# Compressed-cache page loads of a decoder step: eight page numbers per register load, whole pages, pages queued ahead of weight slabs

## The chip, the cores and the metric

One Trainium2 chip, and one of its cores. The metric is device microseconds of the whole program, from launch to the last output, as the median of several runs. A profiled execution of the same program gives the trace from which all rows below are read.

## What is computed

The program is one inference step of a small decoder layer for a prompt of 512 tokens and for 8 sample sequences of 4 tokens, all in float32. The change touches only one part of it: the compressed branch of the sample group's attention, which reads 8 pages of a paged cache per sequence and compresses them with a small network.

```python
def compress(rows, pe, w1, w2):
    halves = pad(rows).reshape(b, nc + 1, CMP_STRIDE, g, d)
    blocks = concatenate([halves[:, :-1], halves[:, 1:]], axis=2) + pe[:, None, :]
    flat = blocks.transpose(0, 1, 3, 2, 4).reshape(b, nc, g, CMP_BLOCK * d)
    return gelu(flat @ w1) @ w2

def full_rows(cache, new):                     # page_table: 8 sequences x 8 pages
    rows = cache[page_table].reshape(b, past, 2, N_KV, HEAD_DIM)
    ...
kc, vc = compress_kv(full_rows(cache_cmp, kv_cmp), pe, w1, w2)
```

A second job of the same stretch is the modulation of the layer's norms, `silu(c) @ w_ada + b_ada`, whose weight comes in 24 slabs of 1 MB. After it come the input projection, the attention, and the feed-forward network, which make up nine tenths of the time.

## The kernel before

Every float32 product is made of three passes on TensorE: a value is split into a high part (ScalarE, `ACTIVATE`) and the remainder (VectorE, `TENSOR_TENSOR`), and high by high, high by low and low by high are added up.

**The sixteen stages.** The loop over `n` (line 553) has 16 stages. Stage `n` works on sequence ("batch") `b = n // 2`, with its keys for even `n` and its values for odd `n`. A batch is 8 pages of 256 KB, one `gt` tile of 2 MB. For a stage, `cmp_split` makes two `xh` tiles on ScalarE and two `xl` tiles on VectorE out of `gt`; `cmp_M` then runs 48 matmuls (`phi`, lines 507 to 509); `cmp_finish` adds the bias on ScalarE (`t`, line 515) and applies gelu (`h`, line 519), and `cmp_out2` makes a small product `ph`. Between stages stand the modulation products `modp` (line 285), each of one slab `ada`, and their transposes `modq`. Ahead of stage 0 stand dummy matmuls (`wake`, line 539) and a bias product `pb` (line 434).

**Tiles.** `gt` tiles have few places: batches 0 and 3 share one, 1 and 4 another, 2, 5 and 7 a third, and batch 6 takes two of the three places for slabs (`raw`). A tile's load can start only when the batch before it in the same place has been split. Weight slabs `phi` and `ada` go through the three `raw` places in turn.

**The SP queue.** All these loads are DMAs issued by SyncE (SP), in one order that is written out by hand: `queue()` (line 208) ties every DMA behind the one before it (`tc.issue_after`), until `ordered` is cleared at stage 11. A page number must be in a register of SP before its page can be issued. `page()` (line 462) loads one number at a time from the SBUF tile `pti`, which has the page table in all 128 partitions, asserts its range, works out the address, and issues the DMA. The DMAs use eight semaphores in turn, so each DMA waits for the landing of the eighth before it. The order is: page table, slab `phi 0`, `hp` (biases, small weights), the first halves (keys) of batch 0's pages, slab `phi 1`, the second halves, `hd`, batch 1, slab `ada 0`, batch 2, slabs `ada 1` and `ada 2`, `xT` (2.2 MB), slab `ada 3`, batch 3, and so on.

**The order on the other engines** is made by a scheduler from the dependences and from its own estimate of times; it isn't written in the code. Each engine then runs its instructions strictly in that order.

Of the kernel before, what the change touches and what calls it, by code (L numbers as in the profile page):

```python
# [142 lines left out]
def build(tc, a, o):  # L143
# [64 lines left out]
    def queue(f):  # L208

        if not ordered[0]:  # L210
            return f()
        if last_q[0] is None:
            last_q[0] = f()
        else:
            with tc.issue_after(last_q[0].ins):
                last_q[0] = f()
        return last_q[0]
# [189 lines left out]
    ptf = mp.tile([128, 64], F32, name="ptf")  # L407
    pm_ = mp.tile([128, 64], F32, name="pm_")
    fidx = mp.tile([128, 8], F32, name="fidx")
    queue(lambda: sync.dma_start(pti, a["page_table"].rearrange("(x b) g -> x (b g)", x=1).broadcast_to([128, 64])))  # L410

    p0 = ExitStack()
    wphip = mkpool(p0, "wphi", side="right")
# [33 lines left out]
    ccv = a["cache_cmp"].rearrange("(n p) w -> n p w", p=128)  # L447
    gb_ = {}

    def cmp_gather(b, vs=(0, 1)):  # L450


        if b not in gb_:
            if b == 6:
                gb_[b] = [raw_tile("gt6").rearrange("p (j w) -> p j w", j=4) for _ in range(2)]
            elif b in (2, 5, 7):
                gb_[b] = [gat.tile([128, 8, 512], F32, tag="gt", bufs=1, name=nm("gt"))]
            else:
                gb_[b] = [hpool.tile([128, KC * NT], F32, tag="h" + "hl"[b in (1, 4)], bufs=1, name=nm("gt"))[:, 0:4096].rearrange("p (j w) -> p j w", j=8)]
        cs = slice(256 * vs[0], 256 * vs[-1] + 256)  # L460

        def page(pg):
            t = gb_[b][pg // 4][:, pg % 4, cs] if b == 6 else gb_[b][0][:, pg, cs]
            r = sync.value_load(pti[0:1, b * 8 + pg:b * 8 + pg + 1], min_val=0, max_val=N_PHYS - 1)
            return sync.dma_start(t, ccv[bass.ds(r, 1)].rearrange("n p w -> (n p) w")[:, cs])

        for pg in range(8):
            queue(lambda: page(pg))

    xst = ExitStack()  # L470
    xp = mkpool(xst, "xp", side="right")
    xT = xbig("xT")
    phi_load(0)
    queue(lambda: sync.dma_start(hp, a["hp"]))
    cmp_gather(0, (0,))
    phi_load(1)
    cmp_gather(0, (1,))
    queue(lambda: sync.dma_start(hd, a["hd"]))
    cmp_gather(1)
    adas = [slab("ada", 0)]  # L480
    cmp_gather(2)
    act.activation(cT[:, :, 0:9], c_in.rearrange("p (k n) -> p k n", k=8), AF.Silu)

    last_hi, last_lo = [None], [None]
# [61 lines left out]
    accs1 = [xp.tile([128, HW[hf]], F32, name=f"xacc{hf}") for hf in range(2)]  # L546
    fin_, mods = None, []
    xs_ = [cmp_split(0, 0, hc) for hc in range(2)]
    wake(2)
    pool.memset(vext[32:64], 0.0)  # L550
    units = []
    AHEAD = {0: (1,), 1: (2,), 2: (3,), 3: (4,), 4: (5,), 5: (6,), 9: (7,)}
    for n in range(16):
        b, v = n // 2, n % 2
        if n == 0:
            with tc.issue_after(last_hi[0].ins):
                for qt in range(4):
# [12 lines left out]
        if n in MODS:  # L570
            mod_slab(MODS.index(n), adas[MODS.index(n)])
        for s_ in AHEAD.get(n, ()):
            adas.append(slab("ada", s_))
        if n == 1:
            queue(lambda: sync.dma_start(xT.rearrange("p k n -> p (k n)"), a["xT"]))
        if n in (2, 4, 6, 8, 11):
            cmp_gather({2: 3, 4: 4, 6: 5, 8: 6, 11: 7}[n])
        if n == 11:
            ordered[0] = False
        if 5 <= n < 9:  # L580
            with tc.issue_after(last_hi[0].ins):
                for k in (2 * n - 10, 2 * n - 9):
                    for hf in range(2):
                        square_acc(xT, k, hf, accs1[hf], xp, k == 0)
        if n == 9:
            invs = [inv_bcast(inv_from_sums(tok_sums(accs1[hf], hf, xp), xp), hf, xp) for hf in range(2)]
        if n == 11:
            modp.pop()()
            make_A(n1T, sc1, A1)
            h = hh_, hl_ = tuple(hpool.tile([128, KC, NT], F32R, tag="h" + n_, bufs=1, name="h_" + n_) for n_ in "hl")  # L590
            units = [u for hf in range(2) for u in [modulate(xT, invs[hf], A1, sh1, hh_, hl_, hf, xp)] * KC]
        for _ in range(3 if n < 15 else 4):
            if units:
# [887 lines left out]
```

## Time and profile before

| | us |
|---|---|
| median of 3 runs (lowest, highest) | 1327.63 (1326.82, 1328.21) |
| the profiled execution, its own time | 1327.7 |
| span from its first to its last instruction | 1325.9 |
| TensorE busy in the span | 1293.4 |
| VectorE busy | 641.5 |
| ScalarE busy | 542.8 |

TensorE is busy for 98% of the span, so a gain must come from where it isn't, or from where it works at its lower clock. The granted clock is given as a share of full speed: 1.00 is 2.4 GHz and 0.50 is 1.2 GHz. Both kinds of loss lie almost wholly in the first 90 us, in the stages above. Outputs of other views name an engine's sequencer with a q (SPq), "PEld" is the loading of weights into TensorE, and "idle before" is the time for which an engine stood still ahead of an instruction, with what ended it.

### The profile page before, as it was taken

What the parts mean: (1) busy time and instruction counts of PE and PEld (TensorE: products, weight loads), DVE (VectorE), ACT (ScalarE), POOL (GpSimd) and SP (SyncE); (2) the same over time, 40 slices, a digit from 0 to 9 for tenths busy, and PEclk for the clock granted to TensorE, in tenths of its full rate; (3) what the DMA queues carried; (4) which work ended last, traced back from release to release, by engine and by line L of the source; (5) the groups of instructions that cost most, each with busy time, mean ns of one, the idle gap of its engine ahead of it and who ended that gap; (6) DMA issues with size and microseconds to landing.
All of it is one profiled execution on the core that took longest, in us unless ns stands there. A gap on an engine that the chain in (4) does not pass through costs nothing.

```text
span 1325.9 us, 26272 instructions
## 1 busy us (share of the span) xinstructions
PE 1293.4 (98%) x10950; PEld 1208.0 (91%) x10950; DVE 641.5 (48%) x1553; ACT 542.8 (41%) x1070; POOL 54.8 (4%) x105
## 2 busy tenths in 40 slices
PE   6999999999999999999999999999999999999997
PEld 4889999998898998998778778999999999999996
DVE  3347632344355454336668576667333333333335
ACT  4346543333232335126677676445323222222223
POOL 1000120001111010001000000000000000000000
PEclk8899999999999999999999999999999999999998
DMA  5975146663755543834536334331123122122211
GB/s 179 360 251 172 68 145 228 223 210 108 278 210 211 223 159 129 210 120 136 150 128 200 108 103 179 127 128 65 64 70 122 64 96 96 56 88 88 88 65 68
DMA packets 43398, 191.39 MB, mean 144 GB/s; under 512 B 4980, under 2 KB 12532, under 8 KB 26904
## 3 DMA queue, kind: packets, MB, share of 16 engines
q1 hardware_dynamic: 40832, 163.52, 36.6%
q0 software_dynamic: 2448, 26.19, 5.1%
q8 instruction: 86, 1.41, 0.4%
q14 instruction: 32, 0.26, 0.1%
HBM read 174.49 MB, written 23.54 MB: 149 GB/s over the span
## 4 chain that ended last, share of the span: by engine, by line
PE 91%; DMA 3%; SPq 2%; DVE 1%; issue 1%; ACT 1%; POOL 0%; POOLq 0%; DVEq 0%; ACTq 0%
PE lin L236 19%; PE lin L237 19%; PE lin L238 19%; PE dn L238 3%; PE dn L236 3%; PE dn L237 3%; PE acc L1164 3%; PE ptp L1170 3%; PE phi L507 2%; PE modp L285 2%; PE phi L508 2%; PE phi L509 2%; DMA wraw<-in_cache_win 2%; PE kt L881 2%; PE sp L1139 1%
## 5 line engine op out<-in xcount | busy, mean ns | idle before, releaser
L232 DVE TENSOR_TENSOR wl<-raw,wh 128x1024 fp32r<-128x1024 f32 (+1 forms) x148 | 178.7, 1207 | 261.4 <-ACT wh L231 260.9
L231 ACT ACTIVATE wh<-raw 128x1024 fp32r<-128x1024 f32 (+1 forms) x148 | 154.9, 1047 | 332.6 <-PE lin L237 238.7
L236 PE MATMUL lin<-h_h,wh 128*128 128x288 f32 x976 | 286.8, 294 | 0.0
L238 PE MATMUL lin<-h_h,wl 128*128 128x288 f32 x976 | 281.4, 288 | 0.0
L237 PE MATMUL lin<-h_l,wh 128*128 128x288 f32 x976 | 280.9, 288 | 0.0
L237 PE MATMUL lin<-h_lo,wh 128*128 128x288 f32 (+1 forms) x672 | 193.9, 289 | 0.0
L238 PE MATMUL lin<-h_hi,wl 128*128 128x288 f32 (+1 forms) x672 | 193.4, 289 | 0.0
L236 PE MATMUL lin<-h_hi,wh 128*128 128x288 f32 (+1 forms) x672 | 192.7, 287 | 0.0
L236 PEld LDWEIGHTS lin<-h_h,wh 128*128 128x128 f32 x976 | 183.8, 188 | 9.5 <-issue 8.3
L237 PEld LDWEIGHTS lin<-h_l,wh 128*128 128x128 f32 x976 | 183.9, 188 | 0.4
L238 PEld LDWEIGHTS lin<-h_h,wl 128*128 128x128 f32 x976 | 183.7, 188 | 0.3
L236 PEld LDWEIGHTS lin<-h_hi,wh 128*128 128x128 f32 x672 | 126.8, 189 | 0.0
L237 PEld LDWEIGHTS lin<-h_lo,wh 128*128 128x128 f32 x672 | 126.5, 189 | 0.2 <-DVE h_lo L361 0.2
L238 PEld LDWEIGHTS lin<-h_hi,wl 128*128 128x128 f32 x672 | 126.1, 188 | 0.0
L236 PE MATMUL dn<-f_hi,wh 128*128 128x256 f32 (+1 forms) x352 | 101.7, 289 | 0.0
L238 PE MATMUL dn<-f_hi,wl 128*128 128x256 f32 (+1 forms) x352 | 101.5, 288 | 0.0
L237 PE MATMUL dn<-f_lo,wh 128*128 128x256 f32 (+1 forms) x352 | 101.1, 287 | 0.0
L507 PE MATMUL phi<-xh,wph 128*128 128x256 f32 x256 | 77.4, 302 | 9.8 <-ACT xh L494 9.8
L508 PE MATMUL phi<-xl,wph 128*128 128x256 f32 x256 | 75.9, 296 | 3.1 <-DVE xl L495 3.1
L1146 ACT ACTIVATE P<-P,nms 128x512 f32<-128x512 f32 (+3 forms) x128 | 70.7, 555 | 19.6 <-DVE nms L1145 18.7
L509 PE MATMUL phi<-xh,wpl 128*128 128x256 f32 x256 | 75.1, 294 | 0.0
L1145 DVE CUSTOM_DVE_ANT_0 P<-sp,ta 128x512 f32<-128x512 f32 (+3 forms) x128 | 57.6, 482 | 30.1 <-PE sp L1133 22.4
(349 smaller groups left out, 2381.6 us busy)
## 6 DMA issues: line engine op xcount, KB each, us to landing
raw<-in_wt SPq DMA_DIRECT2D x98, 1024.0 KB, 4.9
gt<-in_cache_cmp SPq DMA_DIRECT2D x56, 256.0 KB, 3.2
wraw<-in_cache_win POOLq DMA_DIRECT2D x8, 1024.0 KB, 8.7
out_new_win_sample<-in_cache_win SPq DMA_DIRECT2D x8, 512.0 KB, 5.8
out_new_win_sample<-in_cache_win SPq DMA_DIRECT2D x8, 504.0 KB
raw<-in_wt SPq DMA_DIRECT2D x4, 768.0 KB, 4.2
xT<-in_xT SPq DMA_DIRECT2D x1, 2176.0 KB
x<-in_xT SPq DMA_DIRECT2D x1, 2176.0 KB
```

Source lines behind the costliest of these rows:

```text
L231: act.activation(oh, view, AF.Copy)
L232: dve.tensor_sub(ol, view, oh.bitcast(F32))
L236: pe.matmul(p, lhsT=wh[:, k, :], rhs=xh, start=start, stop=False)
L237: pe.matmul(p, lhsT=wh[:, k, :], rhs=xl, start=False, stop=False)
L238: pe.matmul(p, lhsT=wl[:, k, :], rhs=xh, start=False, stop=stop)
L507: pe.matmul(ps_, lhsT=w_h, rhs=mh, start=(ch == 0 and s == 0), stop=False)
L508: pe.matmul(ps_, lhsT=w_h, rhs=ml, start=False, stop=False)
L509: pe.matmul(ps_, lhsT=w_l, rhs=mh, start=False, stop=(ch == 7 and s == 1))
L1145: dve.tensor_tensor_reduce(out=t[:, 0:n], in0=sps[br], in1=t_dist[:, 512 - n:512], scale=-hs, scalar=3e38, op0=ALU.add, op1=ALU.min, accum ...
L1146: act.activation(t[:, 0:n], t[:, 0:n], AF.Exp, scale=-1.0, bias=nms[:, c:c + 1], accum_out=sums[:, c:c + 1])
L1164: pe.matmul(acc[br * 64:br * 64 + 64, :], lhsT=vtok[br][:, j, g * 64:(g + 1) * 64], rhs=pts_[br], start=(j == 0), stop=False)
L1170: pe.transpose(tp[:, r * 128:(r + 1) * 128], P[br, r][:, 128 * j:128 * j + 128], ident)
```

## The change

- `page()` is gone. `cmp_gather` loads the eight page numbers of a batch with one instruction into eight registers, without range assertions.
- The page numbers for this come from a new tile `ptr`, one partition of 64 numbers, loaded first. The broadcast of the table into all 128 partitions (`pti`), which stage 15 still needs, is queued later, behind batch 2.
- Batch 0 is loaded as 8 whole pages, ahead of slab `phi 1`, no longer as 16 half pages around it.
- Batches 3, 4 and 5 are issued at stages 1, 3 and 5 (before: 2, 4 and 6), and ahead of the `ada` slab of the same stage. `xT` is queued at stage 2 (before: 1).
- There is one more dummy matmul (`wake(3)` for `wake(2)`).

```diff
+    ptr = mp.tile([1, 64], I32, name="ptr")
+    ptv = a["page_table"].rearrange("(x b) g -> x (b g)", x=1)
+    queue(lambda: sync.dma_start(ptr, ptv))
...
-        def page(pg):
-            t = gb_[b][pg // 4][:, pg % 4, cs] if b == 6 else gb_[b][0][:, pg, cs]
-            r = sync.value_load(pti[0:1, b * 8 + pg:b * 8 + pg + 1], min_val=0, max_val=N_PHYS - 1)
-            return sync.dma_start(t, ccv[bass.ds(r, 1)].rearrange("n p w -> (n p) w")[:, cs])
-
+        with tc.issue_after(last_q[0].ins):
+            ld, regs = nc.values_load_multi_w_load_instructions(ptr[:, b * 8:b * 8 + 8], [mybir.EngineType.SP], min_val=0, max_val=N_PHYS - 1, skip_runtime_bounds_check_because="a page table names pages of the cache")
+        last_q[0] = ld[-1]
         for pg in range(8):
-            queue(lambda: page(pg))
+            t = ts[pg // 4][:, pg % 4] if b == 6 else ts[0][:, pg]
+            queue(lambda: sync.dma_start(t, ccv[bass.ds(regs[pg], 1)].rearrange("n p w -> (n p) w")))
...
-    cmp_gather(0, (0,))
+    cmp_gather(0)
     phi_load(1)
-    cmp_gather(0, (1,))
     queue(lambda: sync.dma_start(hd, a["hd"]))
     cmp_gather(1)
     adas = [slab("ada", 0)]
     cmp_gather(2)
+    queue(lambda: sync.dma_start(pti, ptv.broadcast_to([128, 64])))
...
-    wake(2)
+    wake(3)
...
-        for s_ in AHEAD.get(n, ()):
-            adas.append(slab("ada", s_))
-        if n == 1:
+        if n in (1, 3, 5, 8, 11):
+            cmp_gather({1: 3, 3: 4, 5: 5, 8: 6, 11: 7}[n])
+        if n in AHEAD:
+            adas.append(slab("ada", AHEAD[n]))
+        if n == 2:
             queue(lambda: sync.dma_start(xT.rearrange("p k n -> p (k n)"), a["xT"]))
-        if n in (2, 4, 6, 8, 11):
-            cmp_gather({2: 3, 4: 4, 6: 5, 8: 6, 11: 7}[n])
```

What this does to the order on the engines is shown at three places. First SP at the start of the program, from the first slab to the first page; `gt_147` and `gt_148` are batch 0's tile. Before:

```order
L222 DMA raw_144<-in_wt 128x2048
L474 DMA hp<-in_hp 128x264
L464 TENSOR_LOAD pti
L464 ISA x2
L465 ISA
L465 DMA gt_147<-in_cache_cmp 128x256
```

With the change:

```order
L222 DMA raw_145<-in_wt 128x2048
L473 DMA hp<-in_hp 128x264
L463 TENSOR_LOAD ptr
L467 ISA
L467 DMA gt_148<-in_cache_cmp 128x512
```

Before, the four rows from the load to the DMA stand for each of the 72 pages and half pages; now the load stands once per batch, and a page has one `ISA` row (the address) and its DMA, which moves 512 columns and not 256.

Second, SP from the last page of batch 2 to the first of batch 3 (`gt_805` and `gt_466`). Before:

```order
L465 DMA gt_394<-in_cache_cmp 128x512
L222 DMA raw_617<-in_wt 128x2048
L222 DMA raw_708<-in_wt 128x2048
L575 DMA xT<-in_xT 128x4352
L222 DMA raw_803<-in_wt 128x2048
L464 TENSOR_LOAD pti
L464 ISA x2
L465 ISA
L465 DMA gt_805<-in_cache_cmp 128x512
```

With the change:

```order
L467 DMA gt_205<-in_cache_cmp 128x512
L480 DMA pti<-in_page_table 128x64
L222 DMA raw_375<-in_wt 128x2048
L463 TENSOR_LOAD ptr
L467 ISA
L467 DMA gt_466<-in_cache_cmp 128x512
```

Between the two batches there were three slabs and `xT`, and there are now the small broadcast and one slab; the other two slabs and `xT` follow behind batch 3.

Third, ScalarE where it passes from the bias and gelu of one stage to the split of a later one. Before, around the split of stage 6 (`xh_1212`, `xh_1216`); `t_78` is the bias of stage 5, which reads the end of that stage's matmuls:

```order
L287 ACTIVATE m_72_1064<-modp_1047 128x128
L515 ACTIVATE t_78_1206<-phi_1153,pbias 128x256
L183 ACTIVATE kcs_91<-ph_77_1202 128x2x63
L519 ACTIVATE h_79_1210<-t_78_1206 128x252
L494 ACTIVATE xh_1212<-gt_805 128x1024
L494 ACTIVATE xh_1216<-gt_805 128x1024
```

With the change, around the split of stage 8 (`xh_1067`, `xh_1071`); `t_105` is the bias of stage 7:

```order
L514 ACTIVATE t_93_982<-phi_927,pbias 128x256
L327 ACTIVATE sq_1002<-xT 128x288
L327 ACTIVATE sq_1005<-xT 128x256
L518 ACTIVATE h_94_986<-t_93_982 128x252
L514 ACTIVATE t_105_1061<-phi_1008,pbias 128x256
L493 ACTIVATE xh_1067<-gt_679 128x1024
L493 ACTIVATE xh_1071<-gt_679 128x1024
```

Before, a stage's split stood behind the end of the stage just ahead of it at stage 6; stage 6 is now split earlier (its `xh` stands ahead of the bias of stage 4), and the place where a split stands behind the end of the stage just ahead of it is stage 8. From stage 13 on, the order on TensorE is the same in both kernels.

## Rows read from the trace of the kernel before

**Rows 1.** The page: busy time of each engine, share of the span, instructions.

```profile
PE 1293.4 (98%) x10950; PEld 1208.0 (91%) x10950; DVE 641.5 (48%) x1553; ACT 542.8 (41%) x1070; POOL 54.8 (4%) x105
```

**Rows 2.** Stages: stretch, length, busy (count) per engine, granted clock, DMA share, GB/s.

```profile
17.30:24.30 7.00, 6.26 (x27) 5.97 (x28) 5.06 (x7) 3.15 (x6) 0.00 (x0) 0.50 0.59 200
...
31.10:38.00 6.90, 6.15 (x27) 5.86 (x28) 2.36 (x2) 1.13 (x3) 0.00 (x0) 0.51 0.83 287
...
44.70:48.30 3.60, 3.60 (x41) 3.22 (x41) 2.30 (x3) 0.94 (x2) 0.00 (x0) 0.53 0.81 303
48.30:75.40 27.10, 27.10 (x298) 25.25 (x296) 7.76 (x18) 7.54 (x14) 0.00 (x0) 1.00 1.01 391
...
79.20:82.40 3.20, 3.12 (x38) 2.42 (x38) 3.09 (x5) 2.89 (x6) 0.00 (x0) 0.51 0.98 341
```

**Rows 3.** TensorE's waits from 0 to 110 us: total, times, longest.

```profile
PE phi L507 <- ACT xh L494: 9.8, 4, 5.5
PE phi L508 <- DVE xl L495: 3.1, 4, 0.9
...
PE ph L527 <- ACT h L519: 1.2, 1, 1.2
PE pbt L441 <- DVE pbs L436: 0.5, 1, 0.5
```

**Rows 4.** TensorE in order of time: start, length, what, idle before and its releaser.

```profile
9.84 1.98 PE L539 MATMUL wake<-ident 128*128 128x512 f32 x4
17.36 0.58 PE L507 MATMUL phi<-xh,wph 128*128 128x256 f32 x1 [5.54 <-ACT xh L494]
...
23.48 0.41 PE L509 MATMUL phi<-xh,wpl 128*128 128x256 f32 x1
23.69 0.41 PE L507 MATMUL phi<-xh,wph 128*128 128x256 f32 x1
...
24.70 0.29 PE L507 MATMUL phi<-xh,wph 128*128 128x256 f32 x1
24.82 0.28 PE L508 MATMUL phi<-xl,wph 128*128 128x256 f32 x1
...
78.02 0.39 PE L507 MATMUL phi<-xh,wph 128*128 128x256 f32 x1 [2.20 <-ACT xh L494]
79.28 0.58 PE L508 MATMUL phi<-xl,wph 128*128 128x256 f32 x1 [0.87 <-DVE xl L495]
...
95.73 0.37 PE L507 MATMUL phi<-xh,wph 128*128 128x256 f32 x1
```

**Rows 5.** SP in order of time: the issues of eight pages (the first two: half pages).

```profile
6.01 8.26 SPq L465 DMA_DIRECT2D gt<-in_cache_cmp  x8
...
15.53 8.70 SPq L465 DMA_DIRECT2D gt<-in_cache_cmp  x8
...
25.48 8.40 SPq L465 DMA_DIRECT2D gt<-in_cache_cmp  x8
```

**Rows 6.** Lines 464 and 465: duration in ns (lowest/median/highest); DMA to landing.

```profile
L464 SPq TENSOR_LOAD <-pti x72: 263/268/476, 5.0 to 120.5; - x72
...
L465 SPq DMA_DIRECT2D gt<-in_cache_cmp x72: 332/333/1219, 6.0 to 121.3; - x72
...
DMA to landing us min/median/max: 2.0/3.2/13.7
```

**Rows 7.** ScalarE and VectorE in order of time, as in rows 4.

```profile
7.84 1.15 ACT L427 ACTIVATE wph<-raw 128x512 fp32r<-128x512 f32 x2 [5.82 <-DMA raw<-in_wt]
...
16.25 2.00 ACT L494 ACTIVATE xh<-gt 128x1024 fp32r<-128x1024 f32 x2 [4.64 <-DMA gt<-in_cache_cmp]
...
17.34 1.23 DVE L495 TENSOR_TENSOR xl<-gt,xh 128x1024 fp32r<-128x1024 f32 x1 [4.93 <-ACT xh L494]
```

**Rows 8.** The DMA view from 48 to 75 us: what was moved.

```profile
DMA packets 2867, 10.56 MB, mean 391 GB/s; under 512 B 319, under 2 KB 319, under 8 KB 2193
```

**Rows 9.** The chain that ended last, its first piece.

```profile
0.75 4.24 DMA pti<-in_page_table
```

More of the change, by code (lines that the diff above doesn't have):

```diff
@@ L409, in build @@
     fidx = mp.tile([128, 8], F32, name="fidx")
-    queue(lambda: sync.dma_start(pti, a["page_table"].rearrange("(x b) g -> x (b g)", x=1).broadcast_to([128, 64])))
+    ptr = mp.tile([1, 64], I32, name="ptr")
+    ptv = a["page_table"].rearrange("(x b) g -> x (b g)", x=1)
+    queue(lambda: sync.dma_start(ptr, ptv))
     p0 = ExitStack()
@@ L448, in build, with cmp_gather @@
     gb_ = {}
[L450 to L460, printed above, removed]
-        def page(pg):
-            t = gb_[b][pg // 4][:, pg % 4, cs] if b == 6 else gb_[b][0][:, pg, cs]
-            r = sync.value_load(pti[0:1, b * 8 + pg:b * 8 + pg + 1], min_val=0, max_val=N_PHYS - 1)
-            return sync.dma_start(t, ccv[bass.ds(r, 1)].rearrange("n p w -> (n p) w")[:, cs])
+    def cmp_gather(b):
+        if b == 6:
+            ts = [raw_tile("gt6").rearrange("p (j w) -> p j w", j=4) for _ in range(2)]
+        elif b in (2, 5, 7):
+            ts = [gat.tile([128, 8, 512], F32, tag="gt", bufs=1, name=nm("gt"))]
+        else:
+            ts = [hpool.tile([128, KC * NT], F32, tag="h" + "hl"[b in (1, 4)], bufs=1, name=nm("gt"))[:, 0:4096].rearrange("p (j w) -> p j w", j=8)]
+        gb_[b] = ts
+        with tc.issue_after(last_q[0].ins):
+            ld, regs = nc.values_load_multi_w_load_instructions(ptr[:, b * 8:b * 8 + 8], [mybir.EngineType.SP], min_val=0, max_val=N_PHYS - 1, skip_runtime_bounds_check_because="a page table names pages of the cache")
+        last_q[0] = ld[-1]
         for pg in range(8):
-            queue(lambda: page(pg))
+            t = ts[pg // 4][:, pg % 4] if b == 6 else ts[0][:, pg]
+            queue(lambda: sync.dma_start(t, ccv[bass.ds(regs[pg], 1)].rearrange("n p w -> (n p) w")))
     xst = ExitStack()
@@ L548, in build @@
     xs_ = [cmp_split(0, 0, hc) for hc in range(2)]
-    wake(2)
+    wake(3)
     pool.memset(vext[32:64], 0.0)
     units = []
-    AHEAD = {0: (1,), 1: (2,), 2: (3,), 3: (4,), 4: (5,), 5: (6,), 9: (7,)}
+    AHEAD = {0: 1, 1: 2, 2: 3, 3: 4, 4: 5, 5: 6, 9: 7}
     for n in range(16):
```

## The prediction

> **What bounds the kernel now.** I read the page first: TensorE is busy for 1293.4 of 1325.9 us [rows 1], so the end moves only by what TensorE is idle or slow. The stage table and TensorE's waits then show where that is. In the first 110 us it waits 9.8 us for `xh`, 3.1 us for `xl`, 1.2 and 0.5 us for small products [rows 3]: 14.6 us. The gaps are 5.54 us ahead of stage 0 and 2.20 + 0.87 us at stage 6 [rows 4]; the rest lies ahead of stages 1 and 2.
>
> The second loss is the clock. In four stretches, 17.3 to 24.3, 31.1 to 38.0, 44.7 to 48.3 and 79.2 to 82.4 us, the granted clock is 0.50 to 0.53, that is the 1.2 GHz level, and each follows one of those gaps [rows 2, 4]. At that level two matmuls of a stage start 0.21 us apart, at 2.4 GHz 0.12 us [rows 4], so 0.43 of the busy time there is lost. Busy are 6.26 + 6.15 + 3.60 + 3.12 = 19.1 us [rows 2]; 0.43 of that is 8.2, and I take 8.0, since the first matmul after a gap is long for another reason. Idle and slow together are 22.6 us. That is all this change can reach.
>
> Why it waits: SP. It issues eight half pages in 8.3 us, eight more in 8.7, then batch 1 in 8.4, one after the other until 33.9 us [rows 5]: 1.1 us a page, of which the DMA itself is 0.33 and the load of its number 0.27 [rows 6]. Batch 1 is the data of stage 2. When SP has slots and the queue is full, the engines move 391 GB/s [rows 8], and 200 to 303 GB/s in the first three slow stretches [rows 2]. So up to stage 5 issue is the limit, not the memory.
>
> **Page numbers.** A page now costs an address and a DMA. Its spacing lies between 0.33 us (the DMA alone) and 1.1 us (as now) [rows 5, 6]; without load (0.27) and assertion, with one address row for three, I take 0.5, nearest to the DMA. One load per batch brings eight numbers. Its price is between 0.27 us, one load, and 8 x 0.268 = 2.14 us [rows 6]; I take the nearer row, one instruction out of SBUF, 0.27. The Trainium skill (Runtime: NRT & Kernel Launch, "Instruction fetch mechanics") speaks against this half of the change: a load costs about 200 ns for each register, in bulk too. By it the load would take an estimated 1.6 us, stage 0 would run some 0.8 us later and the sum would be 1311.8; no run here shows a load of eight.
>
> The saving, about 8 x 0.6 = 5 us of SP per batch, is on the path only until the DMA engines are full. A batch of 2.10 MB takes 5.4 us at 391 GB/s [rows 8], longer than its issue (0.3 + 8 x 0.5 = 4.3). From then on memory sets the pace, and what lies ahead of a page in the queue counts in bytes.
>
> **The table as one row.** The broadcast of 128 rows took 4.24 us and SP stood until 5 us [rows 9]. One row of 256 bytes lands between 2.0 us (the quickest page) and 4.24 us after its issue [rows 6, 9]; I take 2.5, near the quickest, since it is smaller than any page, so the first page goes out at about 3.8 us, for 6.01 now [rows 5]. The broadcast that stage 15 needs is moved behind batch 2, where it can hold the queue for 4.24 us at the most; stage 4 needs batch 2 ten microseconds later, and slab `ada 1` behind it is used in stage 3, some 7 us after it has landed by the sum below, so I put it at nothing.
>
> **Whole pages first.** This has a price: stage 0 needs 1.05 MB of keys, and now waits for 2.10 MB. By issue, the eighth page goes out at 3.8 + 7 x 0.5 = 7.3 us, and lands 3.2 us later [rows 6], at 10.5. By bytes, slab, `hp` and pages are 3.28 MB, 8.4 us at 391 GB/s; from about 2.2 us, 10.6. The slab came at 7.84 [rows 7]; if it is no earlier, pages that wait behind it land at 7.8 + 5.4 = 13.2. If table, load and spacing are all at their slow ends short of today's 1.1 (5 us, 2.14, 0.6), the eighth page is out at 11.6 and lands at 14.8. I take 11.0, for 16.25 now [rows 7]. Then `xh` 1.05 and `xl` 1.23 us [rows 7] give the first two matmuls at 12.1 and 13.3. The values of batch 0 come with it, so stage 1 no longer waits for a second round of loads.
>
> **One more wake.** Two dummies take 1.98 us and end at 11.82 [rows 4]; a third ends at 12.8 and pushes stage 0 there. It costs 0.99 us against the old count of idle time, and leaves about 0.55 us of waiting for `xl` ahead of the second matmul. With so short a gap I expect the clock to stay at 2.4 GHz: after 5.54 us it was down [rows 2, 4].
>
> **Pages ahead of slabs.** Up to and with batch 1 the queue holds 6.5 MB, 16.7 us at 391 GB/s, so batch 1 lands near 19.5 us, where stage 2 wants it at about 27; slab `ada 0` lands near 22, wanted after stage 1 at 26.5; batch 4 (19.25 MB in all) near 54, wanted near 70. Each load has 5 us of cover or more. Batch 3 can be issued early since batch 0's place is free once stage 1 is split, near 20 us. Behind these pages stand slabs whose `raw` place waits for TensorE (`modp`); none is late by this count. ScalarE's order has one place left where a split stands behind the stage before it, now at stage 8 (before: stage 6): I price it as the old one, 2.20 + 0.87 us idle [rows 4] and 0.43 x 3.12 = 1.3 us of slow clock [rows 2], 4.4 us.
>
> **The sum.** Gone: 22.6. New: 0.99 + 0.55 + 4.4 = 5.9. Gain 16.7 us. From the profiled execution's 1327.7 us (span 1325.9, and 1.8 around it) that leaves **1311.0**; the median of the runs, 1327.63, is the same within 0.1. Behind stage 13 TensorE's order is unchanged, its inputs there come from queues that wait for TensorE itself, so I carry the gain to the end.
>
> The Trainium skill (DMA: Bandwidth & Descriptors, "Where 436 GB/s comes from") puts a core's loads from memory at some 358 GB/s. This trace has 391 over 27 us [rows 8], so the measurement decides; by 358 stage 0 would start an estimated 0.8 us later and the sum would be 1311.8.
>
> **Rivals.**
> A, a late start. The first batch lands at 13 to 14.8 us. Then `xl` is ready at 15.5 to 17.1 for 13.3, and after a gap that long the clock falls: 0.43 x 5.5 us, 2.4 as after the old gap. Loss 4.6 to 6.2: 1315.6 to 1317.2; half of it, with the clock held, 1313. For it: the path has four waits in a row (table, load, slab, pages). Against: each has its cheap end nearer. That the change doesn't do what it says belongs here: if the spacing stays 1.1 us, the eighth page goes out at 3.8 + 7.7 = 11.5, lands at 14.7, and the time is 1317; the later batches are still ahead of their stages.
> B, better still. At stage 8 the clock holds, since this is the only gap left: 1.3 us back, and stage 0 starts straight behind the dummies: 1307 to 1309.
> C, given back. Stages 9 to 15 have VectorE and ScalarE work of their own (norm sums, modulation), placed anew. One more split behind its predecessor costs 4.4 us again, two cost 8.8: 1315.4 to 1319.8, and a full return is no change. Against: at 48.3 to 75.4 us TensorE runs through with VectorE busy 7.8 of 27.1 us [rows 2].
> D, slower: the memory doesn't keep up. Stage 8 needs 19.25 MB, and TensorE can't pass it without batch 4. It began at 95.7 us before [rows 4], and break-even is about there. With 2.2 us ahead and 2 us for landing and split, 19.25 MB in 91.5 us is 210 GB/s. Under that rate the change loses; at 200 GB/s, the rate of the first slow stretch [rows 2], stage 8 starts at 100.4 and the time is 1332.4. For it: 200 GB/s is what that stretch shows, with small half pages. Against: SP was issuing there one page per 1.1 us, and with a full queue it is 391.
>
> **How the numbers follow.** Forecast, 1309 to 1313: 0.55. A, 1313 to 1317.2: 0.22. B, 1306.5 to 1309: 0.10. C beyond A, 1317.2 to 1325: 0.07. No change: 0.03. D: 0.03. The likeliest is 1311.0. The range takes the forecast, A and most of B: 1307 to 1317. A measurement here tells 0.2% (2.7 us) from no change; faster 0.94, same 0.03, slower 0.03.
>
> **What would show it.** In the changed trace: one `TENSOR_LOAD` per batch near 0.3 us (2.1 if by register), pages 0.5 us apart, first `xh` near 11 us, first `phi` at 12 to 13 us. Granted clock 1.00 from the start to stage 8, one gap there of about 3 us with a stretch at 0.5 behind it. Rows at 391 GB/s from 5 us on. TensorE's waits for `xh` and `xl` falling from 12.9 us [rows 3] to about 4. The forecast is wrong if `gt` still ends ScalarE's wait past 13 us, if a wait for a slab (`raw`) shows at `modp`, or if TensorE's idle time after stage 9 grows.

## The result, and the profile after

| | before | after |
|---|---|---|
| median, us (lowest, highest; 4 runs each on one chip) | 1327.29 (1326.82, 1328.21) | 1310.88 (1310.23, 1312.21) |
| the profiled execution, us | 1327.7 | 1310.92 |
| its span, us | 1325.9 | 1309.2 |

The ratio is 0.9877, 95% interval 0.986 to 0.9894: the changed kernel is faster by 16.4 us. The forecast was 1311.0. Several terms of its sum were wrong in size, though, and they cancelled; this is worked out in the section on the prediction.

The page of the changed kernel, for the row of [rows 1]:

```profile
PE 1285.6 (98%) x10952; PEld 1201.8 (92%) x10952; DVE 641.9 (49%) x1553; ACT 542.6 (41%) x1070; POOL 54.0 (4%) x105
```

TensorE is busy for 7.8 us less, and idle for 8.9 us less (1309.2 - 1285.6 = 23.6, before 32.5). Its waits from 0 to 110 us after the change (what waited, for what: total us, times, longest), for [rows 3]:

```profile
PE phi L506 <- ACT xh L493: 3.4, 2, 1.9
PE phi L507 <- DVE xl L494: 1.8, 2, 0.9
```

There were 14.6 us of waiting and there are 5.2, at two places. TensorE in order of time (start, length, what, idle before and its releaser), for [rows 4]; the first two are the dummies, then come the starts of stage 0 and stage 8, each with the first matmul that needs `xl`:

```profile
1.47 6.51 PE L538 MATMUL wake<-ident 128*128 128x512 f32 x10 [1.47 <-POOL ident masks.py:199]
...
8.92 2.84 PE L538 MATMUL wake<-ident 128*128 128x512 f32 x6
13.67 0.39 PE L506 MATMUL phi<-xh,wph 128*128 128x256 f32 x1 [1.91 <-ACT xh L493]
14.93 0.38 PE L507 MATMUL phi<-xl,wph 128*128 128x256 f32 x1 [0.87 <-DVE xl L494]
...
73.65 0.38 PE L506 MATMUL phi<-xh,wph 128*128 128x256 f32 x1 [1.51 <-ACT xh L493]
74.91 0.38 PE L507 MATMUL phi<-xl,wph 128*128 128x256 f32 x1 [0.88 <-DVE xl L494]
```

The same stretches by clock (stretch, length, busy with counts of TensorE, its weight loads, VectorE, ScalarE, GpSimd, then granted clock, DMA share, GB/s), for [rows 2, 8]:

```profile
0.00:4.00 4.00, 2.53 (x3) 1.17 (x4) 0.00 (x0) 1.28 (x1) 3.30 (x11) 1.00 0.43 127
4.00:8.00 4.00, 4.00 (x12) 1.53 (x14) 1.17 (x3) 1.81 (x3) 0.14 (x1) 1.00 1.01 359
8.00:12.00 4.00, 3.76 (x38) 1.78 (x38) 1.68 (x4) 1.92 (x4) 0.00 (x0) 1.00 1.06 397
12.00:16.00 4.00, 1.45 (x8) 1.26 (x9) 2.35 (x3) 3.44 (x4) 0.00 (x0) 0.96 1.00 395
15.70:19.10 3.40, 3.40 (x18) 3.40 (x18) 3.40 (x6) 2.84 (x5) 0.00 (x0) 0.50 1.06 389
4.00:60.00 56.00, 53.22 (x525) 46.17 (x523) 27.86 (x46) 27.47 (x42) 0.14 (x1) 0.97 0.99 380
```

One stretch at 1.2 GHz (0.50) is left of four, right behind the gap at stage 0. The DMA engines are full from 4 to 60 us: 380 GB/s, where the kernel before moved 271 in the same stretch:

```profile
4.00:60.00 56.00, 44.53 (x333) 37.46 (x335) 20.21 (x33) 22.01 (x32) 0.15 (x1) 0.82 0.76 271
```

SP in order of time (start, time to the end of the last of the group, what), for [rows 5]:

```profile
0.75 0.34 SPq L412 DMA_DIRECT2D ptr<-in_page_table  x1
1.15 0.37 SPq L222 DMA_DIRECT2D raw<-in_wt  x1
1.56 0.43 SPq L473 DMA_DIRECT2D hp<-in_hp  x1
3.02 4.05 SPq L467 DMA_DIRECT2D gt<-in_cache_cmp  x8
...
9.52 6.33 SPq L467 DMA_DIRECT2D gt<-in_cache_cmp  x8
```

Eight pages go out in 4.05 us; before, eight half pages took 8.26. The next batch takes 6.33 us, because SP stands still for 2.3 us of it, until earlier loads have landed. The line of the load and of the pages (count, duration in ns as lowest/median/highest, first and last start), for [rows 6]:

```profile
L463 SPq TENSOR_LOAD <-ptr x8: 526/530/741, 2.0 to 93.1; - x8
...
L467 SPq DMA_DIRECT2D gt<-in_cache_cmp x64: 332/333/1118, 3.0 to 99.1; - x64
...
DMA to landing us min/median/max: 2.7/5.6/12.7
```

ScalarE and VectorE at the start, for [rows 7]:

```profile
6.17 1.15 ACT L429 ACTIVATE wph<-raw 128x512 fp32r<-128x512 f32 x2 [4.14 <-DMA raw<-in_wt]
...
12.56 2.95 ACT L493 ACTIVATE xh<-gt 128x1024 fp32r<-128x1024 f32 x3 [2.63 <-DMA gt<-in_cache_cmp]
...
13.65 3.50 DVE L494 TENSOR_TENSOR xl<-gt,xh 128x1024 fp32r<-128x1024 f32 x3 [2.71 <-ACT xh L493]
```

Where the time went can be read at one instruction. The first matmul of the input projection (`lin`, line 236) starts at 151.49 us before and at 134.25 us after, 17.24 us earlier; from there to the end it is 1174.4 and 1174.9 us. In the experiments it is 1174.1 to 1175.1, so all of them too are decided ahead of that instruction, to within 1 us.

### The profile page after: what moved, and what is told of

Same layout as the page of the kernel before. It is cut to its first block, busy times and chain, and to the rows that moved or that the text cites. A ratio compares the mean times of both kernels' runs of the same rounds, so it can differ in the third digit from the quotient of the medians.

```text
span 1309.2 us, 26028 instructions
## 1 busy us (share of the span) xinstructions
PE 1285.6 (98%) x10952; PEld 1201.8 (92%) x10952; DVE 641.9 (49%) x1553; ACT 542.6 (41%) x1070; POOL 54.0 (4%) x105
## 4 chain that ended last, share of the span: by engine, by line
PE 93%; DMA 3%; DVE 1%; issue 1%; ACT 1%; POOL 0%; SPq 0%; ACTq 0%; POOLq 0%; DVEq 0%
PE lin L236 19%; PE lin L237 19%; PE lin L238 19%; PE dn L238 3%; PE dn L237 3%; PE dn L236 3%; PE acc L1163 3%; PE ptp L1169 3%; PE phi L506 3%; PE phi L507 2%; PE phi L508 2%; PE modp L285 2%; DMA wraw<-in_cache_win 2%; PE kt L880 2%; PE sp L1138 1%; PE sp L1139 1%
## 5 line engine op out<-in xcount | busy, mean ns | idle before, releaser
L238 PEld LDWEIGHTS lin<-h_hi,wl 128*128 128x128 f32 x672 | 126.1, 188 | 0.0
```

The lines of the kernel that those rows point to most:

```text
L238: pe.matmul(p, lhsT=wl[:, k, :], rhs=xh, start=False, stop=stop)
```

## The experiments

Three groups of runs were made on three chips, and a last kernel on a fourth; the kernel before ran beside each (medians 1328.03, 1327.71, 1327.81 and 1328.03), so kernels of different groups are compared by their ratio to it (the one on record, which is not the quotient of the two medians). "First xh" is the start of ScalarE's first split of batch 0, and "gaps" is TensorE's idle time ahead of the first matmul of a stage and ahead of its first matmul with `xl`.

| kernel | median, us | ratio (95% interval) | first xh | gaps | clock at 0.50 |
|---|---|---|---|---|---|
| changed kernel | 1310.88 | 0.9877 (0.9860 to 0.9894) | 12.56 | stage 0: 1.91 + 0.87; stage 8: 1.51 + 0.88 | 15.7 to 19.1 |
| the same, second group | 1310.17 | 0.9873 (0.9858 to 0.9888) | 12.77 | 0: 1.33 + 0.87; 8: 1.51 + 0.88 | none |
| loads only | 1314.00 | 0.9885 (0.9868 to 0.9901) | 10.05 | 2: 1.50 + 0.88; 6: 2.20 + 0.87 | 28.1 to 34.9, 65.6 to 69.0 |
| order only | 1316.49 | 0.9910 (0.9894 to 0.9927) | 17.22 | 0: 6.17 + 0.46; 8: 1.51 + 0.88 | 14.8 to 25.0 |
| broadcast first | 1314.42 | 0.9897 (0.9880 to 0.9913) | 14.72 | 0: 3.75 + 0.68; 8: 1.51 + 0.88 | 15.7 to 22.5 |
| slabs first | 1313.49 | 0.9886 (0.9870 to 0.9903) | 12.65 | 0: 2.43 + 0.87; 6: 2.49 + 0.68 | 14.8 to 18.2, 62.6 to 69.4 |
| two wakes | 1312.33 | 0.9879 (0.9864 to 0.9894) | 12.51 | 0: 1.94 + 0.83; 8: 1.51 + 0.88 | 13.8 to 20.6, 75.3 to 82.1 |
| halves | 1311.88 | 0.9877 (0.9862 to 0.9892) | 10.21 | 0: 0.87; 1: 0.22; 2: 0.40 + 0.88; 8: 1.51 + 0.87 | 28.5 to 31.9, 76.3 to 79.7 |
| early split of stage 8 | 1305.96 | 0.9843 (0.9830 to 0.9856) | 12.24 | 0: 0.65 + 0.87 | none |
| one number per load | 1312.68 | 0.9886 (0.9871 to 0.9901) | 12.50 | 0: 2.40 + 0.76; 8: 1.51 + 0.87 | 14.6 to 18.0, 76.0 to 79.4 |
| halves and early split | 1307.67 | 0.9847 (0.9834 to 0.9861) | 10.48 | 2: 1.70 + 0.87 | none |
| early split, four wakes | 1307.46 | 0.9849 (0.9836 to 0.9863) | 12.37 | 0: 1.18 + 0.87 | 15.0 to 18.4 |
| early split, six wakes | 1306.29 | 0.9839 (0.9825 to 0.9852) | 12.15 | 0: 0.19 | none |

The changed kernel was run once more in the second group, as the mark for what is compared there:

> The changed kernel once more, as the base for the small effects of the runs beside it: 1310 to 1312 us. It also shows whether the granted clock falls in stage 0 and holds in stage 8 in another execution, after gaps of 1.9 + 0.9 and 1.5 + 0.9 us.

Its median, 1310.17, lies within the runs of the first measurement. Its profiled execution has a shorter gap at stage 0 and no stretch at 0.50, which the last section comes back to.

### The two halves of the change, one at a time

The loads alone: the kernel before with the one-row table and one load of eight numbers per batch (the broadcast goes behind batch 2); batch 0 in halves, the two dummies and the rest of the queue's order stay.

```diff
+    queue(lambda: sync.dma_start(ptr, ptv))
...
+            ld, regs = nc.values_load_multi_w_load_instructions(ptr[:, b * 8:b * 8 + 8], ...)
...
-            r = sync.value_load(pti[0:1, b * 8 + pg:b * 8 + pg + 1], min_val=0, max_val=N_PHYS - 1)
-            return sync.dma_start(t, ccv[bass.ds(r, 1)].rearrange("n p w -> (n p) w")[:, cs])
+            return sync.dma_start(t, ccv[bass.ds(regs[pg], 1)].rearrange("n p w -> (n p) w")[:, cs])
```

> The kernel before with only the loads changed: one-row table first, eight page numbers per load without range checks; batch 0 still in halves, slabs and xT still ahead of batch 3, two dummy matmuls. Theory 1 (the spacing of page issues on SP was the bound, the loads of eight carry the gain): 1307 to 1312 us, first xh near 10 us since keys alone are 1.05 MB, stages 1 and 2 without a long wait, one wait left at stage 6, where ScalarE's order has the split behind stage 5's bias. Rival (the order of pages and slabs and the whole pages carry it): above 1320 us.

The order alone: the changed kernel with one checked load per page out of the broadcast table, which comes first, as before the change; whole pages and the third dummy stay.

```diff
-    queue(lambda: sync.dma_start(ptr, ptv))
+    queue(lambda: sync.dma_start(pti, ptv.broadcast_to([128, 64])))
...
-            ld, regs = nc.values_load_multi_w_load_instructions(ptr[:, b * 8:b * 8 + 8], ...)
...
+            def page():
+                r = sync.value_load(pti[0:1, b * 8 + pg:b * 8 + pg + 1], min_val=0, max_val=N_PHYS - 1)
+                return sync.dma_start(t, ccv[bass.ds(r, 1)].rearrange("n p w -> (n p) w"))
+            queue(page)
```

> The changed kernel with page numbers loaded one by one again, with range checks, out of the broadcast table: only the whole pages, the order of pages and slabs and the third dummy are left of the change. Theory 1: pages again 1.1 us apart, batch 0 lands near 17 us, stage 0 starts near 18 at 1.2 GHz, less waiting ahead of stages 1 and 2 since batch 0 comes in one go: 1316 to 1321 us. Rival (order and whole pages carry the gain): 1311 to 1313 us.

The loads alone gave 14.0 us (1328.03 - 1314.00), the order alone 11.5, both together 16.4 to 17.5. The sum of the parts, 25.5, is far more than the whole: each part removes much of the same waiting. The loads alone lie 2.0 us above their first theory's range and far under the rival's 1320; the order alone lies in its first theory's range. What the order adds to the loads, 2.4 to 3.5 us by the medians, is not clear of the noise: the intervals of the two ratios overlap, and the quickest execution of the loads alone, 1310.72 us at a mean granted clock of 0.998, is as quick as the changed kernel. The traces show which waiting the two parts share. TensorE of the loads alone, at the start of stage 2 and of stage 6:

```profile
27.40 0.39 PE L512 MATMUL phi<-xh,wph 128*128 128x256 f32 x1 [1.50 <-ACT xh L499]
28.66 0.58 PE L513 MATMUL phi<-xl,wph 128*128 128x256 f32 x1 [0.88 <-DVE xl L500]
...
64.36 0.39 PE L512 MATMUL phi<-xh,wph 128*128 128x256 f32 x1 [2.20 <-ACT xh L499]
65.62 0.58 PE L513 MATMUL phi<-xl,wph 128*128 128x256 f32 x1 [0.87 <-DVE xl L500]
```

Stage 0 has almost no gap (0.32 us), but stage 2 waits (its batch goes out behind sixteen half pages, from 15.57 us on, and in the changed kernel from 9.52), and stage 6 waits exactly as in [rows 4]: 2.20 + 0.87 us. That gap belongs to ScalarE's order, which faster loads don't change. TensorE of the order alone, at stage 0:

```profile
18.33 0.58 PE L505 MATMUL phi<-xh,wph 128*128 128x256 f32 x1 [6.17 <-ACT xh L492]
```

Here the long gap at stage 0 is back (it is longer than the 5.54 us of [rows 4]: the first `xh` starts at 17.22 us for 16.25, although the first page goes out at 5.84 for 6.01, since each page brings twice the bytes), and no other gap is left up to stage 8. So whole pages without the cheap loads cost time at stage 0, and the new order removes the gaps of stages 1, 2 and 6 and opens one at stage 8; the loads remove most of that of stage 0, and that of stage 1.

### The table as one row

```diff
-    queue(lambda: sync.dma_start(ptr, ptv))
+    queue(lambda: sync.dma_start(pti, ptv.broadcast_to([128, 64])))
...
-            ld, regs = nc.values_load_multi_w_load_instructions(ptr[:, b * 8:b * 8 + 8], ...)
+            ld, regs = nc.values_load_multi_w_load_instructions(pti[0:1, b * 8:b * 8 + 8], ...)
```

> The changed kernel with the table loaded first as the broadcast into 128 partitions, and the eight-number loads out of that; no second table load. Theory 1: first page near 6 us for 3.0, slab phi 0 near 7.8 for 6.2, so batch 0 lands 1.5 to 2 us later and the clock is low a little longer: 1312.5 to 1314 us. Rival (the late table is hidden, since bytes set batch 0's landing): 1311 us.

SP of this kernel, the first pages:

```profile
5.76 3.97 SPq L466 DMA_DIRECT2D gt<-in_cache_cmp  x8
```

The first page goes out 2.74 us later than after the whole change (3.02), the first `xh` starts 2.16 us later (14.72 for 12.56), and the clock is low for 6.8 us, not 3.4. The median is 3.5 us higher than that of the changed kernel (1314.42 and 1310.88), by the ratios (0.9897 and 0.9877) 2.7 us, and 0.4 us above the first theory's range. The intervals overlap, so the price of the broadcast rests on the trace: the delay at stage 0 and the longer slow stretch.

### One number per load, without range checks

```diff
-        with tc.issue_after(last_q[0].ins):
-            ld, regs = nc.values_load_multi_w_load_instructions(ptr[:, b * 8:b * 8 + 8], ...)
-        last_q[0] = ld[-1]
...
+            with tc.issue_after(last_q[0].ins):
+                ld, regs = nc.values_load_multi_w_load_instructions(ptr[:, b * 8 + pg:b * 8 + pg + 1], ...)
+            last_q[0] = ld[-1]
```

> The changed kernel, but with one load per page number (out of the one-row table, still without range assertion): it separates eight numbers per load from the missing assertions. Theory 1 (from the eighth page on, bytes set the pace: pages landed 0.65 us apart in the changed kernel although they were issued 0.52 us apart): a page costs 0.52 + 0.27 - 0.07 = 0.72 to 0.8 us of SP, the eighth page goes out at about 8.3 us for 6.7, the first xh moves from 12.5 to 13 to 13.7 us, later stages do not wait more, and the time is 0.5 to 1.2 us above the changed kernel's 1310.2 to 1310.9: 1310.7 to 1312. Theory 2 (eight numbers per load are what pays, the assertions cost little): a page costs near 1.1 us again, the first xh comes at 15 to 16 us, stage 2 waits as well, and the time is 1313 to 1316.

SP, then ScalarE, of this kernel:

```profile
2.75 6.19 SPq L467 DMA_DIRECT2D gt<-in_cache_cmp  x8
...
12.50 3.90 ACT L493 ACTIVATE xh<-gt 128x1024 fp32r<-128x1024 f32 x4 [2.70 <-DMA gt<-in_cache_cmp]
```

A page costs 0.83 us of SP (the eighth goes out at 8.61), between 0.52 and 1.13 (from the first 8.26 us of [rows 5]): of the 0.61 us that a page saved, dropping the assertions gave some 0.30 and the grouping 0.31. The first `xh` is not a bit later (12.50 for 12.56), although the eighth page goes out 1.9 us later than in the changed kernel (6.70): the issue is not what sets the landing of batch 0. The second theory, that the grouping pays, falls at this row, and the first had its `xh` at 13 to 13.7 us, too late as well. The median, 1312.68, is 0.7 us above the first theory's range, and its interval overlaps that of the changed kernel. In the profiled execution the clock fell at stage 0 and at stage 8, in the changed kernel's at stage 0 alone; the second fall, 0.43 x 3.40 = 1.5 us, is more than the 0.9 us by which the two spans differ (1310.1 and 1309.2). So eight numbers at a time, the first thing that the change names, is worth nothing that these runs can show; what is left of the loads, the missing assertions and the one-row table, is the part that counted. No run has the assertions together with the one-row table, so the two are not told apart.

### Pages behind the slabs, and two wakes

```diff
-        if n in (1, 3, 5, 8, 11):
-            cmp_gather({1: 3, 3: 4, 5: 5, 8: 6, 11: 7}[n])
...
-        if n == 2:
+        if n == 1:
...
+        if n in (2, 4, 6, 8, 11):
+            cmp_gather({2: 3, 4: 4, 6: 5, 8: 6, 11: 7}[n])
```

> The changed kernel with batches 3, 4 and 5 and xT queued at their old stages, behind the slabs. Theory 1: every load has 5 us of cover, the order is worth nothing by itself; the one split behind its predecessor is at stage 6 and not at stage 8: 1310 to 1312.5 us. Rival (the pages ahead of slabs matter): stage 6 or 8 waits for its pages, 1315 us or more.

With the later batches back in their old places, the gap is at stage 6 again:

```profile
62.78 0.58 PE L506 MATMUL phi<-xh,wph 128*128 128x256 f32 x1 [2.49 <-ACT xh L493]
64.04 0.58 PE L507 MATMUL phi<-xl,wph 128*128 128x256 f32 x1 [0.68 <-DVE xl L494]
...
62.60:69.40 6.80, 5.94 (x48) 4.95 (x49) 6.12 (x10) 5.20 (x12) 0.00 (x0) 0.50 0.70 247
```

The last line is the stretch behind it: 6.8 us at 1.2 GHz, while the changed kernel has its gap at stage 8 and ran there at full clock. The median is 2.6 us above the changed kernel's, by the ratios 1.2, with intervals that overlap, and lies between the ranges of the two theories. This part of the change therefore moves a gap of ScalarE's order from stage 6 to stage 8, and makes it smaller (2.39 for 3.17 us); it did not remove it. Behind the gap at stage 6 the clock fell in all three kernels that have it (before, loads only, slabs first), behind that at stage 8 in three profiled executions of seven.

```diff
-    wake(3)
+    wake(2)
```

> The changed kernel with two dummy matmuls for three. Theory 1 (the landing of batch 0 sets the start of stage 0, the dummy fills a gap): TensorE's gap ahead of stage 0 is 2.9 us for 1.9, the start is the same, the clock falls sooner or as soon: 0 to 1 us slower than the changed kernel. Rival (a dummy pushes stage 0, as the prediction's sum had it): 1.0 us faster.

Without the third dummy stage 0 starts at 13.6 us, as with it. The third dummy is not on the path: 1312.33 against 1310.17 in the same group (2.2 us, more than the 0 to 1 of the first theory, but the intervals overlap), with the clock low for 6.8 us at stage 0 and again at stage 8.

### Batch 0 in halves

```diff
+        if b == 0:
+            for pg in range(8):
+                queue(lambda: sync.dma_start(ts[0][:, pg, 0:256], ccv[bass.ds(regs[pg], 1)].rearrange("n p w -> (n p) w")[:, 0:256]))
+            phi_load(1)
+            for pg in range(8):
+                queue(lambda: sync.dma_start(ts[0][:, pg, 256:512], ccv[bass.ds(regs[pg], 1)].rearrange("n p w -> (n p) w")[:, 256:512]))
+            return
...
-    phi_load(1)
```

> The changed kernel with batch 0 in half pages again, keys ahead of slab phi 1 and values behind it, all with the eight registers of one load. Theory 1 (bytes set the landing of batch 0): keys land near 9.5 us for 12.5, stage 0 runs from 11.8 us, the gap ahead of it all but closes and the clock holds: 3 to 4 us faster than the changed kernel. Rival (sixteen issues and small rows hold the queue, or the values come late for stage 1): within 1 us of it or slower.

The first theory, 3 to 4 us faster, falls. Half the bytes do bring the first `xh` to 10.21 us, 2.56 earlier than in the same group's changed kernel, and the dummies run into stage 0. But eight more DMAs push batch 1 back (its first page goes out at 16.29 us for 9.24), and stage 2 waits; the time stays (0.9877 against 0.9873). With the split of stage 8 made early as well (this diff and that of the next section in one kernel):

> The changed kernel with both additions at once: batch 0 in halves (keys ahead of slab phi 1, values behind it), and the split of stage 8 ahead of the bias of stage 7 on ScalarE. Theory 1 (the loads of the first 30 us are limited by bytes, so that what the halves give at stage 0 is waited for again at stage 2): the start of stage 0 near 11.5 us, a wait of 0.4 + 0.9 us at stage 2, none at stage 8, and the time within 1.5 us of the early split alone (1306.0): 1304.5 to 1307.5. Theory 2 (the gain of the halves at stage 0, 2.3 us, was hidden in the run with halves alone by the slow clock at stage 8): the two gains add up, and the time is 1303 to 1304.4.

TensorE and ScalarE of that kernel at stage 2:

```profile
27.12 2.95 ACT L499 ACTIVATE xh<-gt 128x1024 fp32r<-128x1024 f32 x3 [3.00 <-DMA gt<-in_cache_cmp]
...
28.23 0.39 PE L512 MATMUL phi<-xh,wph 128*128 128x256 f32 x1 [1.70 <-ACT xh L499]
29.49 0.39 PE L513 MATMUL phi<-xl,wph 128*128 128x256 f32 x1 [0.87 <-DVE xl L500]
```

ScalarE waits 3.00 us for batch 1 there, and TensorE 2.57, more than the 1.52 us that the early split alone (below) still waits at stage 0. The median is 1307.67, with the first theory (0.2 us above its range) and 3.3 us above the upper end of the second: what whole pages cost at stage 0 they give back at stage 2.

### The split of stage 8 ahead of the bias of stage 7

In the changed kernel ScalarE takes the bias of stage 7, which needs the end of that stage's matmuls, and only then splits for stage 8 (the third order block ahead of the prediction). Here the split comes first:

```diff
-        fin_ = cmp_finish(b, v, po)
-        if n < 15:
+        if n == 7:
+            xs_ = [cmp_split((n + 1) // 2, (n + 1) % 2, hc) for hc in range(2)]
+            with tc.issue_after(last_hi[0].ins):
+                fin_ = cmp_finish(b, v, po)
+        else:
+            fin_ = cmp_finish(b, v, po)
+        if n < 15 and n != 7:
```

> The changed kernel with stage 8's split ahead of stage 7's bias on ScalarE. Theory 1 (the wait at stage 8 is only ScalarE's order; the pages landed long before): the 1.5 + 0.9 us ahead of stage 8 go, 2.2 to 2.6 us faster than the changed kernel. Rival (the bias of stage 7, now later, holds TensorE through its small product or its PSUM place): the wait comes back at another place, within 0.5 us of it.

ScalarE around this place, first in the changed kernel (two lines), then with the early split:

```profile
72.18 0.47 ACT L514 ACTIVATE t<-phi,pbias 128x256 f32<-128x256 f32 x1 [4.20 <-PE phi L508]
72.55 1.99 ACT L493 ACTIVATE xh<-gt 128x1024 fp32r<-128x1024 f32 x2
...
66.07 2.01 ACT L493 ACTIVATE xh<-gt 128x1024 fp32r<-128x1024 f32 x2
70.37 0.47 ACT L514 ACTIVATE t<-phi,pbias 128x256 f32<-128x256 f32 x1 [2.29 <-PE phi L508]
```

In the changed kernel ScalarE stands for 4.20 us with batch 4 in SBUF and nothing to do but wait for TensorE; with the early split it uses that time. TensorE's waits of this kernel from 0 to 110 us:

```profile
PE phi L507 <- DVE xl L494: 0.9, 1, 0.9
PE phi L506 <- ACT xh L493: 0.6, 1, 0.6
```

The gap at stage 8 is gone, and the median is 1305.96, 4.2 us under the changed kernel of the same group; the intervals of the ratio (0.9830 to 0.9856 and 0.9858 to 0.9888) don't touch. I had expected 2.2 to 2.6. In the two profiled executions `lin` starts 3.4 us earlier (129.53 for 132.96): 2.39 us are the gap, 0.5 a stage 0 that began earlier (13.35 for 13.87 us), and 0.5 other work between stages 7 and 9. The rest lies in executions that were not profiled; those of the changed kernel went from 1309.11 us (mean granted clock 0.997) to 1312.40 (0.995), so a slow stretch in some of them is the likely cause, and that is argued, not shown.

### More dummies, to keep the clock

```diff
-    wake(3)
+    wake(4)
```

> The early split of stage 8 with four dummy matmuls ahead of stage 0 for three. Theory 1 (stage 0 starts when the split of batch 0 is ready, at 13.5 us, and the dummies end before that): the fourth takes 0.43 to 0.85 us out of the gap ahead of stage 0 and does not move its start; time within 1 us of the early split with three (1306.0), and the clock stays at 1.00 at stage 0. Theory 2 (the dummies set the start of stage 0, as the prediction of the change took it): stage 0 starts 0.43 to 0.99 us later and the time is 1306.4 to 1307.0 if the clock holds as before.

```diff
-    wake(3)
+    wake(6)
```

> The early split of stage 8 with six dummy matmuls ahead of stage 0, so that the dummies reach the split of batch 0 wherever the clock rises: with four they ended at 12.3 us, 1.2 us ahead of it, and the clock fell at 15.0 to 18.4 us. Theory 1 (the fall at stage 0 comes with the gap ahead of it): the dummies end at 13.1 to 13.8 us, the gap ahead of the first product of stage 0 is 0 to 0.4 us, the clock stays at 1.00 to the end of the stages, and the time is 1.5 us under the four dummies' 1307.5, less up to 0.4 us for a start that is pushed: 1305.7 to 1306.5. Theory 2 (the fall has nothing to do with the length of that gap): the clock falls again at 14 to 16 us and the time is 1307.4 to 1308.2.

Both kernels have the early split of stage 8. TensorE with four dummies, then with six:

```profile
8.60 3.70 PE L538 MATMUL wake<-ident 128*128 128x512 f32 x8
13.48 0.39 PE L506 MATMUL phi<-xh,wph 128*128 128x256 f32 x1 [1.18 <-ACT xh L493]
14.74 0.38 PE L507 MATMUL phi<-xl,wph 128*128 128x256 f32 x1 [0.87 <-DVE xl L494]
...
8.80 5.42 PE L538 MATMUL wake<-ident 128*128 128x512 f32 x12
13.65 0.68 PE L506 MATMUL phi<-xh,wph 128*128 128x256 f32 x1
14.52 0.39 PE L507 MATMUL phi<-xl,wph 128*128 128x256 f32 x1 [0.19 <-DVE xl L494]
```

The granted clock right behind, four dummies and six:

```profile
15.00:18.40 3.40, 3.40 (x18) 3.40 (x18) 3.40 (x5) 3.35 (x6) 0.00 (x0) 0.50 1.05 387
...
13.60:17.00 3.40, 3.21 (x23) 2.67 (x22) 3.40 (x4) 3.40 (x6) 0.00 (x0) 1.00 1.03 381
```

With four, stage 0 starts where it did, as the first theory had it, but the clock, against it, fell, and the median, 1307.46, lies above the ranges of both theories. With six the gap ahead of the first matmul is closed, stage 0 starts at 13.65 us, within the 13.35 to 13.87 of the changed kernel and of the early split with three dummies, and the clock holds at 1.00 to the end of the stages. The median is 1306.29, in the range of the first theory. The clock of the executions that were not profiled agrees: its mean is 0.996 in all five with four dummies, and 0.997 or 0.998 in all five with six. These five runs lie within 0.7 us (1306.14 to 1306.87), those with three dummies within 2.3 (1305.68 to 1307.93, on another chip). Six dummies don't beat three in the median (0.9839 and 0.9843). Either of the two beats both kernels of this case: 0.9839 (0.9825 to 0.9852) is 21.7 us under before.

## Why the prediction came out right, and where its steps were wrong

**What bounds the kernel.** Right. Only idle and slow TensorE ahead of `lin` moved the end, and only 0.5 us was given back behind it (1174.4 and 1174.9 us).

**Page numbers.** The spacing of pages was right (0.52 us measured, 0.5 forecast). The load of eight took 0.53 us: not one load's 0.27 that I chose, and far from eight loads' 2.14. One load is 0.268 us [rows 6], so each further register added (0.530 - 0.268) / 7 = 0.037 us. The price per register that the Trainium skill states (Runtime: NRT & Kernel Launch, "Instruction fetch mechanics") does not hold for this load out of SBUF; by it I had estimated 1.6 us, but the page gives it beside the register loads of a program's preamble.

**The table as one row.** Better than forecast: the load of the numbers starts at 2.0 us and the first page goes out at 3.02, for 3.8. With the broadcast it is 5.76. Moved behind batch 2, the broadcast delayed nobody: no wait of TensorE lies between stage 0 and stage 8.

**Whole pages first.** This is the first step that failed. The first `xh` came at 12.56, for 11.0 forecast, although the eighth page was out at 6.70 and not at 7.3. I had named the bound by bytes (10.6 us at 391 GB/s from 2.2 us on) and then taken almost that. The windows show what was left out: 127 GB/s up to 4 us and 359 up to 8 us, and by 12.41 us, when the last page lands, 0.51 + 1.44 + 1.59 + 0.16 = 3.70 MB have been moved, for 3.28 of the slab, `hp` and the pages. So 0.42 MB of what is queued behind them (slab `phi 1`, `hd`, batch 1) shared the engines with them, another 1.1 us at 397 GB/s. Here the landing was not set by the bytes queued ahead of it alone, once the engines were full.

**One more wake.** The second step that failed, and in both numbers. I took a dummy at 0.99 us, and two (four rows) do take 1.98 before [rows 4]; but the three end at 11.76 us and not at 12.8, because they began at 8.92 for 9.84: at the start of the program the first ten rows took 6.51 us for 7.43. Stage 0 was not pushed; it waited 1.91 + 0.87 us, where I had 0.55. The run with two wakes shows the same.

**The clock at stage 0.** Also wrong: after this gap it fell, at 0.43 x 3.40 = 1.5 us. That was a piece of rival A, at a price under A's, since the batch landed before 13 us.

**Stage 8.** The place was right, the price not: 1.51 + 0.88 = 2.39 us for 3.07, and the clock held in the profiled execution, so the 1.3 us of slow clock were not paid there. With two wakes, with halves and with one number per load the same gap of 1.51 + 0.87 or 0.88 us was followed by a slow stretch.

**The sum.** The new losses were 0.86 (the added dummy: 2.84 for 1.98) + 2.78 + 1.5 + 2.39 = 7.5 us, for 5.9 forecast. That alone would have given 1312.6. The span shrank by 16.7 us and not by 22.6 - 7.5 = 15.1: another 0.9 us came from the first dummies (6.51 for 7.43), which I had not in the sum. The last 0.7 us comes from a term of the old loss that was too small, the 8.0 us of slow clock. TensorE up to the first `lin`, before, after, and in the second execution of the changed kernel, which has no stretch at 0.50:

```profile
0.00:151.49 151.49, 135.48 (x1217) 120.96 (x1217) 79.06 (x182) 75.61 (x134) 3.75 (x15) 0.92 0.63 219
...
0.00:134.25 134.25, 127.61 (x1218) 114.78 (x1218) 80.13 (x182) 76.44 (x136) 3.74 (x15) 0.99 0.66 246
...
0.00:132.96 132.96, 126.90 (x1218) 113.57 (x1218) 80.14 (x182) 76.45 (x136) 3.74 (x15) 1.00 0.68 249
```

Without the dummies (9.41, 9.35 and 10.13 us) TensorE is busy for 126.1, 118.3 and 116.8 us. So the slow clock cost 9.3 us before, and 1.5 us after, as priced above. Of the 1.3 us by which 8.0 was too little, 0.5 were lost again behind `lin`; that leaves 0.8, and the account closes to 0.1 us. The forecast of 1311.0 was met because stage 0 with its dummy cost 3.6 us more than forecast (5.14 for 1.54), and stage 8 (2.0), the first dummies (0.9) and this rest (0.7) gave 3.6 back. That these errors cancelled was luck. The mechanism was right: cheaper issue and the new order remove TensorE's gaps and the slow clock behind them.

**The rivals.** D is out: 380 GB/s over 56 us. C is out too: no wait of TensorE appears between stage 8 and `lin`. Half of A (the late gap, the fallen clock) and half of B (the clock held at stage 8) happened in the same execution.

**Memory.** The 391 GB/s of the trace of before held: 389 to 397 with a full queue. The 358 of the Trainium skill (DMA: Bandwidth & Descriptors, "Where 436 GB/s comes from") is again passed.

## What to carry to other kernels

When two parts of a change remove the same waiting, their gains don't add: price them on one common list of gaps, and look for the gap that neither touches, here a split queued on ScalarE behind an instruction that waited for TensorE. Making the issue of a load cheaper pays until the engines are full; from there what counts is how many bytes, of this load and of those issued behind it, are in flight before it lands. And where two errors of a sum can cancel, check the terms one by one in the new trace, not the total.

## What the runs showed of the hardware that I had not expected

- The clock after a gap is not the same in every execution. The gap of 1.51 + 0.87 to 0.88 us at stage 8 was followed by full clock in four profiled executions (the changed kernel twice, order only, broadcast first) and by 1.2 GHz in three (two wakes, halves, one number per load). At stage 0, 1.33 + 0.87 us was followed by full clock and 1.18 + 0.87 us by the lower one. At stage 2, 0.40 + 0.88 us was followed by the lower level (halves) and 1.70 + 0.87 us by full clock (halves and early split). A prediction should carry both outcomes, here 1.5 us apart for a stretch of 3.4 us; runs of one kernel differed by up to 4.3 us, and the quicker had the higher mean granted clock (loads only: 1310.72 us at 0.998, 1314.99 at 0.993).
- The first dummies, the same code in every kernel, took from 5.95 us (one number per load) to 7.59 (loads only). They start 0.85 us apart at first and 0.43 us apart later, two to one like the two levels of the clock, and what differs is when the pace changes: at 5.4 us in the first profiled execution of the changed kernel, at 7.0 us in the second. The trace's record of the granted clock begins at the same moments, with 1.00; the 1.00 that the windows show for the time before is no measurement. In these two executions the first dummies took 6.51 and 7.29 us; behind the quicker ones the gap ahead of stage 0 was 1.91 us and the clock fell, behind the slower ones it was 1.33 us and the clock held. Time won at the dummies is waited for at stage 0, and can cost the clock there. In all six executions in which the pace changed before 5.5 us and stage 0 waited 1.18 + 0.87 us or more, the clock fell there; where it changed at 7.0 us or later, it held after 0.65 + 0.87 (early split) and 1.33 + 0.87 us, and fell after 1.94 + 0.83 (two wakes) and 5.54 + 0.68 us (before). Why is not shown.
- A register load of eight neighbouring numbers took 0.53 us, twice that of one.
